# Storing the last rows of a transformer step from 128 partitions: the sample's output as one folded tile

## The chip, the cores and the metric

The kernel runs on one core of one Trainium2 chip. The metric is the device time of one execution in microseconds (us), as a median of several runs. The profile is of one further execution.

## The reference

One layer of a hybrid encoder step is computed for 256 prompt frames and 64 sample frames of width 2048, all in float32. Only its last step bears on the change: the final normalisation of both streams.

```python
def _rmsnorm(x, g):
    xf = x.astype(jnp.float32)
    y = xf * lax.rsqrt(jnp.mean(xf * xf, axis=-1, keepdims=True) + EPS)
    return (y * g.astype(jnp.float32)).astype(x.dtype)
...
    y_prompt = _rmsnorm(xp, final_norm_g)   # (1, 256, 2048)
    y_sample = _rmsnorm(xs, final_norm_g)   # (1, 64, 2048)
```

Before it stand the input projection, the gated branch, the attention branch, the merge and a feed-forward block of 5632 columns. Each output row is 2048 floats, 8 KB.

## The kernel before

The 256 + 64 frames are handled as one block of T = 320 tokens. All large products keep the features on the partitions and the tokens in the free dimension: a weight block of 128x128 is the stationary side, 320 tokens are the moving side, and each weight is split into a high and a low part, so that three products are made for each block (L168 to L170). Weights come from DRAM by the sync queue, ScalarE makes the high part (L135), VectorE the low one (L144). A small calendar (`later`, `pump`) places side work between the products.

The last products are those of w_ffn_down, in column blocks (`DOWN`). The result x2 is kept in `f1` as 16 blocks (m = 0 to 15) of 128 features by 320 tokens. For blocks 0 to 13 the calendar runs, between later products: `out_square` (sum of squares in `acc`), `out_gain` (times final_norm_g) and `out_turn`, which transposes the block on TensorE to token rows (`turn_out`, L895) and copies them from a PSUM bank to the tile `tok` (L908, L909). `tok` is 128 partitions by 3 row groups by 2048 features: row groups 0 and 1 are prompt frames 0 to 127 and 128 to 255, row group 2 holds the 64 sample frames in partitions 0 to 63. `xs` is the list of the three row groups with their heights, (0, 128), (1, 128), (2, 64).

From L941 on the order is written out by hand. `sum_up` (L947) sums the squares over the partitions by a product with a column of ones, for each row group into a PSUM bank of its own, in three calls: for `acc`, for block 14, for block 15. Blocks 14 and 15 are turned in between, their copies to `tok` are made by ScalarE (L905, L906). `sfs` (L969) takes the sums from PSUM to SBUF, and ScalarE's square root with a correction step on VectorE makes `r3`, one factor for each row and row group (L970 to L974).

`scale_out` (L977 to L984) then multiplies a piece of `tok` by its column of `r3`, on VectorE (L983) or ScalarE (L981), and stores it to DRAM on the sync queue or the scalar queue. The order is: row group 0 in two quarters of 512 columns (VectorE, sync queue), first half of row group 1 (ScalarE, scalar queue), first half of the sample (VectorE, sync queue), second half of row group 0 (VectorE, sync queue), second half of row group 1 (ScalarE, scalar queue), second half of the sample (VectorE, scalar queue). These are seven stores. The sync engine waits at the end of the program for all of them (shown as L1043).

Of the kernel before, what the change touches and what calls it, by code (L numbers as in the profile page):

```python
# [12 lines left out]
AF = mybir.ActivationFunctionType  # L13
ALU = mybir.AluOpType
# [4 lines left out]
P = 128  # L19
D = 2048  # L20
DC = D // P
T = 320
TS = 64
F = 5632
FC = F // P
W = 512
EPS = 1e-6
# [43 lines left out]
def tile_hybrid_step(ctx: ExitStack, tc: tile.TileContext, a: dict, outs: list):  # L71
    nc = tc.nc
    y_p, y_s, ko_p, vo_p, ko_s, vo_s, gv_s = outs
# [10 lines left out]
    def bank(name):  # L84
        return psum.tile([P, 512], F32, tag="bank", name=name)
# [94 lines left out]
    ident = main.tile([P, P], F32, name="ident")  # L180
    make_identity(nc, ident)
    ones = main.tile([P, P], F32, name="ones")
# [4 lines left out]
    tok = main.tile([P, 3, D], F32, name="tok")  # L187
# [6 lines left out]
    xs = [(i, P if i < 2 else TS) for i in range(3)]  # L194
# [585 lines left out]
    for g in range(4):  # L780
        ps = gemm(w_bb, g * W, yh, yl, f"bb{g}")
        for t in range(4):
            m = 4 * g + t
# [48 lines left out]
    for g in range(4):  # L832
        ps = gemm(w_ba, g * W, yh, yl, f"ba{g}")
        for t in range(4):
            m = 4 * g + t
# [21 lines left out]
    for g in range(4):  # L857
        ps = gemm(w_out, g * W, xh, xl, f"wo{g}")
        for t in range(4):
            m = 4 * g + t  # L860
# [30 lines left out]

    def turn_out(m, src):
        pt = bank(f"y_{m}")
        for i, n in xs:
            nc.tensor.transpose(pt[:n, i * P : (i + 1) * P], src[:, i * P : i * P + n], ident)  # L895
        return pt

    def out_turn(m, pt=None):
        c = slice(m * P, (m + 1) * P)
        act = pt is not None  # L900
        if not act:
            pt = turn_out(m, f1[:, m, :])
        pv = pt[:, 0:256].rearrange("p (i c) -> p i c", i=2)
        if act:
            nc.scalar.activation(tok[:, 0:2, c], pv, AF.Copy)  # L905
            nc.scalar.activation(tok[0:64, 2, c], pt[0:64, 256:384], AF.Copy)  # L906
        else:
            nc.vector.tensor_copy(tok[:, 0:2, c], pv)  # L908
            nc.vector.tensor_copy(tok[0:64, 2, c], pt[0:64, 256:384])  # L909

    f0 = 0
    for nf in FPARTS:
        for g in range(nf // 4):
            c0 = f0 * P + g * W
            ps = gemm(w_fg, c0, yh, yl, f"fg{f0 + 4 * g}")
            sg = tmp.tile([P, 4, T], F32, tag="st", name=f"sg_{f0 + 4 * g}")
            for t in range(4):
                nc.vector.tensor_tensor(sg[:, t, :], ps[t], r2, op=ALU.mult)
                nc.scalar.activation(sg[:, t, :], sg[:, t, :], AF.Silu)
            ps = gemm(w_fu, c0, yh, yl, f"fu{f0 + 4 * g}")  # L920
            for t in range(4):
                e = tmp.tile([P, T], F32, tag="e1", name=f"h_{f0 + 4 * g + t}", bufs=4)
                nc.vector.tensor_tensor(e, ps[t], r2, op=ALU.mult)
                later(1 + t, lambda m=4 * g + t, e=e, s=sg[:, t, :]: act(m, e, s))
        last = f0 + nf == FC
        for c0, nt in DOWN[last]:
            ps = gemm(w_fd, c0, xh, xl, f"fd{f0}_{c0}", k0=f0, nk=nf, nt=nt)
            if last and c0 == (DC - 2) * P:
                break
            for t in range(nt):  # L930
                m = c0 // P + t
                nc.vector.tensor_tensor(f1[:, m, :], ps[t], f1[:, m, :], op=ALU.add)
                if last:
                    later(1 + 2 * t, lambda m=m: out_square(m))
                    later(1 + 2 * t, lambda m=m: out_gain(m))
                    later(2 + 2 * t, lambda m=m: out_turn(m))
        f0 += nf
# [2 lines left out]

    ctx.enter_context(tc.manual_schedule())  # L941
    lp = late["pool"]
    pss = [bank(f"pss_y_{i}") for i in range(3)]

    def sum_up(q, j):
        for i, n in xs:
            nc.tensor.matmul(  # L947
                pss[i][:n, 0:2], q[:, i * P : i * P + n], ones[:, 0:2], start=(j == 0), stop=(j == 2)
            )

    sfs = lp.tile([P, 3], F32, name="sfs")
    r3 = lp.tile([P, 3], F32, name="r3")
    nh = lp.tile([P, 3], F32, name="nh")
    nc.vector.memset(sfs, 1.0)
    nc.scalar.activation(scrap, acc[:, 0:1], AF.Sqrt)
    sum_up(acc, 0)
    pts = []
    for j, m in enumerate((DC - 2, DC - 1)):
        x2 = f1[:, m, :]
        nc.vector.tensor_tensor(x2, ps[j], x2, op=ALU.add)  # L960
        sq = tmp.tile([P, T], F32, tag="e1", name=f"ysq_{m}", bufs=4)
        nc.scalar.activation(sq, x2, AF.Square)
        xg = tmp.tile([P, T], F32, tag="e1", name=f"xg_{m}", bufs=4)
        nc.vector.tensor_scalar_mul(xg, x2, vec[:, 48 + m : 49 + m])
        sum_up(sq, 1 + j)
        pts.append(turn_out(m, xg))
    out_turn(DC - 2, pts[0])
    for i, n in xs:
        nc.vector.tensor_scalar(sfs[:n, i : i + 1], pss[i][:n, 0:1], 1.0 / D, EPS, op0=ALU.mult, op1=ALU.add)  # L969
    nc.scalar.activation(r3, sfs, AF.Sqrt)  # L970
    nc.vector.reciprocal(r3, r3)
    nc.vector.tensor_tensor(nh, sfs, r3, op=ALU.mult)
    nc.vector.scalar_tensor_tensor(nh, nh, -0.5, r3, ALU.mult, ALU.mult)
    nc.vector.scalar_tensor_tensor(r3, nh, 1.5, r3, ALU.add, ALU.mult)  # L974
    out_turn(DC - 1, pts[1])

    def scale_out(i, c, eng, queue):  # L977
        n = xs[i][1]
        y = tok[:n, i, c]
        if eng is nc.scalar:  # L980
            nc.scalar.activation(y, y, AF.Copy, scale=r3[:n, i : i + 1])  # L981
        else:
            nc.vector.tensor_scalar_mul(y, y, r3[:n, i : i + 1])  # L983
        queue.dma_start(y_p[0][i * P : (i + 1) * P, c] if i < 2 else y_s[0][:, c], y)  # L984

    h0, h1 = slice(0, D // 2), slice(D // 2, D)
    scale_out(0, slice(0, D // 4), nc.vector, nc.sync)
    scale_out(0, slice(D // 4, D // 2), nc.vector, nc.sync)
    scale_out(1, h0, nc.scalar, nc.scalar)
    scale_out(2, h0, nc.vector, nc.sync)  # L990
    scale_out(0, h1, nc.vector, nc.sync)
    scale_out(1, h1, nc.scalar, nc.scalar)
    scale_out(2, h1, nc.vector, nc.scalar)


# [51 lines left out]
```

## Time and profile before

| what | us |
|---|---|
| median of 3 runs | 1952.28 (1951.65 to 1952.33) |
| the profiled execution, its own time | 1951.71 |
| its span, first to last instruction | 1949.8 |
| granted TensorE clock, mean | 0.997 |

The time of an execution is its span and 1.9 us around it. In the rows further down PE is TensorE (products), PEld its weight loads, DVE is VectorE, ACT is ScalarE; a "q" behind an engine's name is its instruction queue, on which DMA issues and waits stand. All times are counted from the start of the span.

### The profile page before, as it was taken

To read this page: it belongs to the slowest core of one execution; us is meant where nothing else is said; L and a number is where in the kernel's file an instruction comes from. 1 tells how busy PE (TensorE), PEld (TensorE's weight loads), DVE (VectorE), ACT (ScalarE), POOL (GpSimd) and SP (SyncE) were. 2 spreads that over 40 slices of the span, in tenths; PEclk is the share of its full clock that TensorE was granted. 3 is DMA by queue.
4 is the path that set the end of the run, shared out by engine and by line. 5 is a ranking of instruction groups with operands and counts; after the bars stand their busy time and mean duration, and the time that the engine had idled before them with its cause. 6 is when DMAs were issued, how large, how long until landed. Compare 5 with 4: busy or idle time off the path is not lost.

```text
span 1949.8 us, 31855 instructions
## 1 busy us (share of the span) xinstructions
PE 1930.4 (99%) x13207; PEld 1924.3 (99%) x13207; DVE 1042.9 (53%) x1530; ACT 813.4 (42%) x1219; POOL 4.7 (0%) x12
## 2 busy tenths in 40 slices
PE   9999999999999999999999999999999999999997
PEld 9999999999999999999999999999999999999997
DVE  6878887944355544455454444443444444444455
ACT  6666766532233343334443333332333333333343
POOL 0000000000000000000000000000000000000000
PEclk9999999999999999999999999999999999999999
DMA  8566566744444444445445555445555544555443
GB/s 279 158 174 179 163 187 180 223 155 149 149 141 135 146 148 149 149 151 205 151 144 150 151 151 152 152 149 146 150 151 151 152 151 148 146 151 151 152 132 106
DMA packets 171024, 307.41 MB, mean 158 GB/s; under 512 B 11472, under 2 KB 31392, under 8 KB 170688
## 3 DMA queue, kind: packets, MB, share of 16 engines
q1 hardware_dynamic: 166128, 295.67, 49.7%
q10 hardware_dynamic: 4752, 9.72, 1.7%
q8 instruction: 103, 1.69, 0.4%
q14 instruction: 41, 0.34, 0.0%
HBM read 292.15 MB, written 12.45 MB: 156 GB/s over the span
## 4 chain that ended last, share of the span: by engine, by line
PE 92%; DVE 2%; ACT 2%; DMA 2%; issue 1%; SPq 0%; ACTq 0%; DVEq 0%
PE mm_fg L170 5%; PE mm_fd L170 5%; PE mm_fu L170 5%; PE mm_fd L169 5%; PE mm_fu L169 5%; PE mm_fg L169 5%; PE mm_fg L168 5%; PE mm_fu L168 5%; PE mm_fd L168 5%; PE mm_u L168 2%; PE mm_bb L169 2%; PE mm_bb L170 2%; PE mm_ba L168 2%; PE mm_ga L168 2%; PE mm_wo L168 2%; PE mm_wo L169 2%
## 5 line engine op out<-in xcount | busy, mean ns | idle before, releaser
L144 DVE TENSOR_TENSOR lo<-raw,hi 128x1024 fp32r<-128x1024 f32 (+1 forms) x533 | 645.3, 1211 | 660.8 <-ACT hi L135 659.4
L135 ACT ACTIVATE hi<-raw 128x1024 fp32r<-128x1024 f32 (+1 forms) x533 | 559.3, 1050 | 1008.7 <-PE mm_fu L169 188.6
L168 PE MATMUL mm_fd<-xh,hi 128*128 128x320 f32 x704 | 218.2, 310 | 0.0
L168 PE MATMUL mm_fg<-yh,hi 128*128 128x320 f32 x704 | 217.8, 309 | 0.0
L170 PE MATMUL mm_fg<-yh,lo 128*128 128x320 f32 x704 | 217.5, 309 | 0.0
L168 PE MATMUL mm_fu<-yh,hi 128*128 128x320 f32 x704 | 217.5, 309 | 0.0
L169 PE MATMUL mm_fu<-yl,hi 128*128 128x320 f32 x704 | 217.5, 309 | 0.0
L170 PE MATMUL mm_fu<-yh,lo 128*128 128x320 f32 x704 | 217.5, 309 | 0.0
L169 PE MATMUL mm_fg<-yl,hi 128*128 128x320 f32 x704 | 217.5, 309 | 0.0
L170 PE MATMUL mm_fd<-xh,lo 128*128 128x320 f32 x704 | 217.1, 308 | 0.0
L169 PE MATMUL mm_fd<-xl,hi 128*128 128x320 f32 x704 | 217.1, 308 | 0.0
L168 PEld LDWEIGHTS mm_fg<-yh,hi 128*128 128x128 f32 x704 | 132.1, 188 | 0.1
L169 PEld LDWEIGHTS mm_fg<-yl,hi 128*128 128x128 f32 x704 | 132.1, 188 | 0.1
L170 PEld LDWEIGHTS mm_fg<-yh,lo 128*128 128x128 f32 x704 | 132.1, 188 | 0.0
L168 PEld LDWEIGHTS mm_fu<-yh,hi 128*128 128x128 f32 x704 | 132.1, 188 | 0.0
L169 PEld LDWEIGHTS mm_fu<-yl,hi 128*128 128x128 f32 x704 | 132.1, 188 | 0.0
L170 PEld LDWEIGHTS mm_fu<-yh,lo 128*128 128x128 f32 x704 | 132.1, 188 | 0.0
L169 PEld LDWEIGHTS mm_fd<-xl,hi 128*128 128x128 f32 x704 | 132.1, 188 | 0.0
L168 PEld LDWEIGHTS mm_fd<-xh,hi 128*128 128x128 f32 x704 | 132.1, 188 | 0.0
L170 PEld LDWEIGHTS mm_fd<-xh,lo 128*128 128x128 f32 x704 | 132.1, 188 | 0.0
L168 PE MATMUL mm_q<-xh,hi 128*128 128x320 f32 x256 | 81.2, 317 | 0.0
L168 PE MATMUL mm_u<-xh,hi 128*128 128x320 f32 x256 | 80.3, 314 | 0.0
(267 smaller groups left out, 3933.0 us busy)
## 6 DMA issues: line engine op xcount, KB each, us to landing
raw<-in_w_in_dram SPq DMA_DIRECT2D x103, 512.0 KB
raw<-in_w_ffn_gate_dram SPq DMA_DIRECT2D x88, 512.0 KB
raw<-in_w_ffn_up_dram SPq DMA_DIRECT2D x88, 512.0 KB
raw<-in_w_ffn_down_dram SPq DMA_DIRECT2D x82, 512.0 KB
raw<-in_w_gate_dram SPq DMA_DIRECT2D x64, 512.0 KB
raw<-in_w_branch_b_dram SPq DMA_DIRECT2D x32, 512.0 KB
raw<-in_w_branch_a_dram SPq DMA_DIRECT2D x32, 512.0 KB
raw<-in_w_out_dram SPq DMA_DIRECT2D x32, 512.0 KB
```

What stands on the lines that cost most here:

```text
L135: nc.scalar.activation(hi[:, :, :n], raws[j][:, :, :n], AF.Copy)
L144: nc.vector.tensor_tensor(lo[:, :, :n], raws.pop(j)[:, :, :n], f32(parts[j][0][:, :, :n]), op=ALU.subtract)
L168: nc.tensor.matmul(o, hi[:, c, cols], xh[:, k, :], start=(k == 0), stop=False)
L169: nc.tensor.matmul(o, hi[:, c, cols], xl[:, k, :], start=False, stop=False)
L170: nc.tensor.matmul(o, lo[:, c, cols], xh[:, k, :], start=False, stop=(k == nk - 1))
```

## The change

The sample's features 1024 to 2047 go to partitions 64 to 127 of row group 2 of `tok`, beside features 0 to 1023 in partitions 0 to 63. To get them there, `turn_out` transposes for the blocks m = 8 to 15 the tokens 192 to 319 (128 columns, whose upper 64 are the sample) in place of tokens 256 to 319, and the copies in `out_turn` take partitions 64 to 127 of the bank to partitions 64 to 127 of `tok`. `sum_up` makes a fourth group of sums for the tokens 192 to 319 in a fourth bank, so that the factors of the sample are in `sfs` in partitions 64 to 127 too; the memset of `sfs` is gone. The sample is scaled by one VectorE operation of 128x1024 instead of two of 64x1024. It is stored in two pieces of 128 partitions by 512 columns, the first on the sync queue, the second on the scalar queue; the target of each is the output seen as (h t d), with h = 2 halves of the features.

```diff
     def turn_out(m, src):
         pt = bank(f"y_{m}")
-        for i, n in xs:
-            nc.tensor.transpose(pt[:n, i * P : (i + 1) * P], src[:, i * P : i * P + n], ident)
+        for i in range(2):
+            nc.tensor.transpose(pt[:, i * P : (i + 1) * P], src[:, i * P : (i + 1) * P], ident)
+        s0 = 2 * P - m // 8 * TS
+        nc.tensor.transpose(pt[: T - s0, 2 * P : 3 * P], src[:, s0:T], ident)
         return pt
 
     def out_turn(m, pt=None):
+
         c = slice(m * P, (m + 1) * P)
+        r = slice(m // 8 * TS, m // 8 * TS + TS)
+        cs = slice(m % 8 * P, m % 8 * P + P)
...
-            nc.scalar.activation(tok[0:64, 2, c], pt[0:64, 256:384], AF.Copy)
+            nc.scalar.activation(tok[r, 2, cs], pt[r, 256:384], AF.Copy)
         else:
             nc.vector.tensor_copy(tok[:, 0:2, c], pv)
-            nc.vector.tensor_copy(tok[0:64, 2, c], pt[0:64, 256:384])
+            nc.vector.tensor_copy(tok[r, 2, cs], pt[r, 256:384])
...
-    pss = [bank(f"pss_y_{i}") for i in range(3)]
+    pss = [bank(f"pss_y_{i}") for i in range(4)]
 
     def sum_up(q, j):
-        for i, n in xs:
-            nc.tensor.matmul(
-                pss[i][:n, 0:2], q[:, i * P : i * P + n], ones[:, 0:2], start=(j == 0), stop=(j == 2)
-            )
+        for o, c in zip(pss, (0, P, 2 * P, T - P)):
+            n = min(P, T - c)
+            nc.tensor.matmul(o[:n, 0:2], q[:, c : c + n], ones[:, 0:2], start=(j == 0), stop=(j == 2))
...
-    nc.vector.memset(sfs, 1.0)
...
-    for i, n in xs:
-        nc.vector.tensor_scalar(sfs[:n, i : i + 1], pss[i][:n, 0:1], 1.0 / D, EPS, op0=ALU.mult, op1=ALU.add)
+    for i, r in ((0, slice(0, P)), (1, slice(0, P)), (2, slice(0, TS)), (3, slice(TS, P))):
+        nc.vector.tensor_scalar(
+            sfs[r, min(i, 2) : min(i, 2) + 1], pss[i][r, 0:1], 1.0 / D, EPS, op0=ALU.mult, op1=ALU.add
+        )
...
+    def scaled(i, c, eng):
+        y = tok[:, i, c]
+        if eng is nc.scalar:
+            nc.scalar.activation(y, y, AF.Copy, scale=r3[:, i : i + 1])
+        else:
+            nc.vector.tensor_scalar_mul(y, y, r3[:, i : i + 1])
+        return y
+
     def scale_out(i, c, eng, queue):
-        n = xs[i][1]
-        y = tok[:n, i, c]
-        if eng is nc.scalar:
-            nc.scalar.activation(y, y, AF.Copy, scale=r3[:n, i : i + 1])
-        else:
-            nc.vector.tensor_scalar_mul(y, y, r3[:n, i : i + 1])
-        queue.dma_start(y_p[0][i * P : (i + 1) * P, c] if i < 2 else y_s[0][:, c], y)
+        queue.dma_start(y_p[0][i * P : (i + 1) * P, c], scaled(i, c, eng))
...
     scale_out(1, h0, nc.scalar, nc.scalar)
-    scale_out(2, h0, nc.vector, nc.sync)
+    sample = scaled(2, h0, nc.vector)
+    dst = y_s[0].rearrange("t (h d) -> h t d", h=2)
+    nc.sync.dma_start(dst[:, :, 0:W], sample[:, 0:W])
     scale_out(0, h1, nc.vector, nc.sync)
     scale_out(1, h1, nc.scalar, nc.scalar)
-    scale_out(2, h1, nc.vector, nc.scalar)
+    nc.scalar.dma_start(dst[:, :, W : 2 * W], sample[:, W : 2 * W])
```

## Rows read from the trace of the kernel before

**Rows 1.** The page, busy time and share of the span of each engine; granted clock.
```profile
span 1949.8 us, 31855 instructions
PE 1930.4 (99%) x13207; PEld 1924.3 (99%) x13207; DVE 1042.9 (53%) x1530; ACT 813.4 (42%) x1219; POOL 4.7 (0%) x12
PEclk9999999999999999999999999999999999999999
```

**Rows 2.** Chain of waits, its end: start, length, work.
```profile
1937.24 0.56 PE pss_y L947 x6
...
1937.83 0.16 DVE sfs L969
...
1938.01 0.21 ACT r L970
...
1939.05 0.49 DVE tok L983
...
1939.93 1.98 DVE tok L983 x3
```

**Rows 3.** Waits of the sync engine's queue, 1938 to 1949.8: total, times, longest.
```profile
SPq L984 <- DVE tok L983: 17.0, 3, 16.1
SPq L1043 <- DMA out_dram<-tok: 6.2, 3, 3.3
```

**Rows 4.** DMA view, 1940.3 to 1948.6, in 40 slices of 0.21 us; q1 sync, q10 scalar.
```profile
DMA  3999999999999999999498789999989989798520
GB/s 148 375 365 405 375 415 355 484 395 395 375 415 375 316 296 237 237 158 158 99 237 336 316 336 513 375 375 454 434 336 434 454 296 375 217 237 237 197 99 0
DMA packets 880, 2.62 MB, mean 316 GB/s; under 512 B 112, under 2 KB 112, under 8 KB 880
q1 hardware_dynamic: 512, 1.31, 50.9%
q10 hardware_dynamic: 368, 1.31, 43.9%
```

**Rows 5.** Table of stretches: length, busy time by engine, clock, DMA share, GB/s.
```profile
1941.90:1943.00 1.10, 0.00 (x0) 0.00 (x0) 0.01 (x1) 0.00 (x0) 0.00 (x0) 0.50 1.03 395
1943.20:1944.40 1.20, 0.00 (x0) 0.00 (x0) 0.00 (x0) 0.00 (x0) 0.00 (x0) 0.50 1.04 201
1944.60:1947.00 2.40, 0.00 (x0) 0.00 (x0) 0.00 (x0) 0.00 (x0) 0.00 (x0) 0.50 0.97 384
1947.20:1948.20 1.00, 0.00 (x0) 0.00 (x0) 0.00 (x0) 0.00 (x0) 0.00 (x0) 0.50 0.88 238
1948.60:1949.80 1.20, 0.00 (x0) 0.00 (x0) 0.00 (x0) 0.00 (x0) 0.00 (x0) 0.50 0.00 0
```

**Rows 6.** DMA view, 240 to 249: scalar queue's packets, its copies.
```profile
q10 hardware_dynamic: 64, 0.16, 4.8%
...
swp<-qr ACTq DMA_DIRECT2D x4, 40.0 KB
```

**Rows 7.** DMA view, 1940.4 to 1941.7.
```profile
DMA packets 257, 0.49 MB, mean 380 GB/s; under 512 B 16, under 2 KB 16, under 8 KB 257
q1 hardware_dynamic: 257, 0.49, 102.0%
```

**Rows 8.** DMA view, 1942 to 1943.
```profile
DMA packets 96, 0.39 MB, mean 393 GB/s; under 512 B 0, under 2 KB 0, under 8 KB 96
```

**Rows 9.** Timeline, 1934.6 to 1938.5: start, length, engine, line, operation, [idle before].
```profile
1934.63 0.49 DVE L960 TENSOR_TENSOR f<-mm_fd,f 128x320 f32<-128x320 f32 x1 [2.03 <-PE mm_fd L170]
1935.17 0.76 PEld L947 LDWEIGHTS pss_y<-ones,acc 128*128 128x128 f32 x6
1935.51 0.49 DVE L960 TENSOR_TENSOR f<-mm_fd,f 128x320 f32<-128x320 f32 x1
1936.69 0.55 PE L895 MATMUL y<-ident,xg 128*128 128x128 f32 x3
1936.97 0.73 PEld L947 LDWEIGHTS pss_y<-ones,ysq 128*128 128x128 f32 x6
1937.39 0.58 DVE L969 TENSOR_SCALAR sfs<-pss_y 128x1 f32<-128x1 f32 x3 [0.97 <-PE pss_y L947]
```

**Rows 10.** Groups by line and shape, 1868 to 1934: busy us, mean ns.
```profile
L895 PE MATMUL y<-ident,f 128*128 128x128 f32 x28 | 5.3, 272 | 0.0
L895 PEld LDWEIGHTS y<-ident,f 128*128 128x128 f32 x28 | 3.9, 140 | 0.1
L895 PE MATMUL y<-ident,f 128*64 128x128 f32 x14 | 3.8, 272 | 0.0
L895 PEld LDWEIGHTS y<-ident,f 128*64 128x64 f32 x14 | 1.5, 110 | 0.0
```

**Rows 11.** Groups by line and shape, 1938 to 1949.8: busy us, mean ns.
```profile
L983 DVE TENSOR_SCALAR tok<-tok,r 64x1024 f32<-64x1024 f32 x2 | 1.5, 742 | 0.0
L983 DVE TENSOR_SCALAR tok<-tok,r 128x1024 f32<-128x1024 f32 x1 | 0.7, 743 | 0.0
```

**Rows 12.** Timeline, 1939 to 1949.8: ScalarE's second scaling, the queues' DMA issues.
```profile
1939.56 2.93 SPq L984 DMA_DIRECT2D out_dram<-tok  x4
1940.62 1.15 ACT L981 ACTIVATE tok<-tok,r 128x1024 f32<-128x1024 f32 x1 [0.43 <-ACT tok L981]
1941.80 1.51 ACTq L984 DMA_DIRECT2D out_dram<-tok  x2
```

## The prediction

> **What bounds the kernel now.** I read the page first: TensorE is busy for 99% of a 1949.8 us span at full clock [rows 1], and nothing in the change touches the products that fill it. So the change can move the time only in the end, after the last product, and, by a hair, through the transposes in the last products. I went to the end with the chain of waits: it leaves TensorE at 1937.8, runs through the small root chain (sfs, r3) to 1939.0, then through VectorE's scaling operations of L983 [rows 2]. Behind these no engine computes anything; the reader should see that the sync engine's own waits end on the stores of tok, 6.2 us of them [rows 3]. So the end of the program is the landing of the stores, and the question is what the 16 DMA engines do between 1940.4 and 1948.5.
>
> The DMA view of that stretch [rows 4] tells three things. First, all seven stores lie in it: 2.62 MB. Second, of its 880 packets 112 are under 512 B. The rows stored are 128+128+64+128 on the sync queue (448) and 128+128+64 on the scalar queue (320), together 768 data packets, one for each row; 880 - 768 = 112 = 7 x 16. So each store leaves one small closing packet on each DMA engine that it used, and each of the seven used all 16. Third, the rate falls twice, to 99 GB/s in the middle and again at the end, while elsewhere it is near 390.
>
> The table of stretches says where [rows 5]: while the 128-row store of the scalar queue runs alone (1941.9 to 1943.0), 395 GB/s; while the sample's first half runs, a store from partitions 0 to 63 alone, 201 GB/s with the engines as busy as before (1.04); in the last microsecond, with the sample's second half, 238. From 1948.6 on nothing moves, and the program closes in 1.2 us. So 64-partition stores are dear: 262,144 B at 201 GB/s is 1.30 us, at 395 it would be 0.66. This is what the change goes for.
>
> **The change, part by part.** The two sample stores become two stores of 128 SBUF rows of 2 KB each. Their target is written as (h t d): outermost h, with 2 values, then 64 rows t, then 512 floats. Outermost counts are thus 128 on the SBUF side and 2 on the DRAM side. **The decisive unknown is over how many DMA engines such a store is dealt.** No transfer of this trace has unlike outermost counts at its two ends. The nearest rows are the rope exchanges at 240 to 249 us: four copies of 8 partitions, 40 KB each [rows 6]. They leave 64 packets on the scalar queue; 4 x 8 rows are 32 data packets, so 32 closing packets, 8 for each copy. An outermost count of 8 is dealt over 8 engines; 64 and 128 over 16. If a share is an equal cut of the outermost count at both ends, 128 and 2 have only two shares in common: partitions 0 to 63 with h=0, and 64 to 127 with h=1. I therefore take **2 engines**, and, as both stores have one shape, the same two for both; the other end of the range is 16.
>
> The Trainium skill states this rule outright (DMA: Bandwidth & Descriptors, section "Why a DMA increments its semaphore by 16 and not by 1"): the engine count is the largest number up to 16 that divides the slowest dimension of both patterns, and the engines are the lowest-numbered ones. By it both sample stores would sit on the same two engines, and the result would be the forecast below; by the rows alone it would be either that or one of the rivals.
>
> Prices of a packet on one engine. A 2 KB packet: in 1940.4 to 1941.7 the quarter stores keep 16 engines full (102%) and start 257 packets, 16 of them closing ones [rows 7]; 16 x 1.3 us / 241 = 0.086 us. A 4 KB packet: 96 packets in 1942.0 to 1943.0 [rows 8], 16 x 1.0 / 96 = 0.167 us. Bounds for the 2 KB one: half of the 4 KB one, 0.083, and 0.086.
>
> Load of the two engines after the change, if both sample stores fall on the same pair: two quarter stores, 8 + 8 packets of 2 KB, 16 x 0.086 = 1.4; three stores of 512 KB, 8 packets of 4 KB each, 24 x 0.167 = 4.0; the sample's, 64 + 64 packets of 2 KB, 128 x 0.086 = 11.0. Sum **16.4 us**. Before, every engine had 16 x 0.086 + 32 x 0.167 = 6.7 us of work at these prices and took 8.1 (1940.4 to 1948.5), the rest being the slow 64-row packets. So the stores last **+8.3 us** longer. The other 14 engines have 5.4 us of work and finish far earlier.
>
> Where the stores start: sum_up runs for four row groups, not three. Three groups are six weight loads in 0.73 us [rows 9], 0.12 each; two more in each of three calls is 6 x 0.12 = +0.73. They are on the path: TensorE goes from one call to the next without a pause, from 1935.17 to 1937.80, and sfs waits for the last. The fourth sfs operation costs 0.58/3 = 0.19 at most [rows 9]; it is partly covered by waiting for the last sum, I take 0.1 (0 to 0.19). The transposes of the sample load 128 columns, not 64, for 8 of the 16 turns: 140 against 110 ns, the operation itself 272 either way [rows 10]; 8 x 0.03 = +0.2 on a full TensorE.
>
> Edits at nothing: the memset of sfs (VectorE waits 2.0 us for the last product there [rows 9]; without that cover some 0.16); one scaling less on VectorE (0.74 by the 64-row form; 128 rows take 0.743 too [rows 11]): ScalarE's second scaling ends at 1940.62 + 1.15 = 1941.8 [rows 12], and the engines have stores until 1948.5 that hide it. The fourth bank of sums makes 8 with two products and two turned blocks; should a turned block get a product's bank, that one is free after L960 at 1936.0, before the transposes at 1936.69 [rows 9].
>
> Queues: behind the sample's first half on the sync queue stands the 512 KB store of (0, h1); if its issue is held until 64 packets on one engine drain, the two engines have the scalar queue's rows meanwhile, so nothing; without that cover the price is the time from issue to first packet, 1939.56 to 1940.4 [rows 4, 12], 0.84 us, twice at most (1.7). The sample's second half on the scalar queue no longer waits for a later scaling; it stands behind (1, h1) as before.
>
> Sum: 8.3 + 0.73 + 0.1 + 0.2 = **+9.3 us**. The profiled execution took 1951.71, its span 1949.8 with 1.9 around it; the median of the runs, 1952.28, lies 0.6 above it. On the median: **1961.6**. Its own range: 2 KB packets at 0.083 (-0.4) and start terms of 0.5 instead of 1.0 give 1960.6; two uncovered issues give 1963.4.
>
> **The rivals.**
> (a) The stores are dealt over all 16 engines, and the change does what it says: not slower. This decides if the SBUF side alone, 128 rows, sets the shares. For it: every 128-row store of the end does so [rows 4]. Against it: the DRAM side has only two outer blocks. Then each sample store gains 1.30 - 0.66 = 0.64, the last one, by 238 GB/s, 1.10 - 0.66 = 0.44: -1.1 against +1.0 at the start: 1952.2, no change that can be told.
> (b) Two engines for each store, but different pairs. The trace cannot tell which eight engines the rope copies took. Then the fullest engine has 1.4 + 4.0 + 64 x 0.086 = 10.9, +2.8 over 8.1, and with 1.0: +3.8, 1956.1.
> (c) Two engines, and the held queue is not covered: 1963.4, in the forecast's range.
>
> **How the numbers follow.** The forecast with (c) 0.80, (b) 0.05, (a) 0.13, anything else 0.02. About 0.2% (3.9 us) is what a measurement of this kernel can tell from no change: slower is above 1956.2. Slower: the forecast and part of (b), 0.82; same: (a) and the rest of (b), 0.17; faster 0.01, since even all of the 8.1 us of stores holds only 1.4 us above the packets' price. The range reaches from (b) to a little over (c): 1955.8 to 1963.8.
>
> **What the profile after would show.** Right: in the stretch of the stores fewer closing packets, 5 x 16 + 2 x 2 = 84 small ones against 112; 384 KB on each of two engines, seen as a long tail at about 2 x 24 = 48 GB/s for some 8 to 10 us after a short stretch near 390; a store end near 1957.7 and a span near 1959. The sums: eight loads of L947 for each call, and L983 starting some 0.8 us later. Wrong: 112 small packets, or a tail at twice that rate (then (b)), or a tail as long with all engines busy, which would mean slow packets and not few engines.

## The result, and the profile after

The changed kernel takes 1960.93 us (median of 6 runs) against 1951.97 for the kernel before in the same sets: the ratio is 1.0049, with a 95% interval of 1.0036 to 1.0061. It is slower by some 9 us; the prediction was 1961.6, in a range of 1955.8 to 1963.8.

Two lines of the page; the span was 1949.8 before [rows 1]:

```profile
span 1958.6 us, 31867 instructions
PE 1930.0 (99%) x13213; PEld 1923.7 (98%) x13213; DVE 1042.9 (53%) x1529; ACT 813.7 (42%) x1219; POOL 4.7 (0%) x12
```

TensorE did the same work, to 0.4 us. The waits of the sync engine's queue (total, times, longest) grow where the end waits for the stores, from 6.2 us [rows 3] to:

```profile
SPq L1052 <- DMA out_dram<-tok: 15.2, 3, 12.4
```

The DMA view of the stretch that holds all seven stores, 1940.1 to 1957.4, in 40 slices of 0.43 us; it answers to [rows 4]:

```profile
DMA  9999999999896412011111111111111111111110
GB/s 346 379 398 431 398 369 379 350 350 341 322 417 265 114 47 33 9 38 33 38 47 52 52 52 52 52 47 52 52 52 52 47 52 57 57 47 47 52 52 28
DMA packets 980, 2.62 MB, mean 152 GB/s; under 512 B 84, under 2 KB 84, under 8 KB 980
```

The bytes are the same, 2.62 MB. The small packets are 84 and no longer 112: five stores closed on 16 engines and two on 2 each, 5 x 16 + 2 x 2. For 5.6 us the stores run near 370 GB/s; then, after one slice at 114, come some 11 us below 60, most of them between 47 and 57, with a busy share of 1 in 10. The table of stretches (length, busy time by engine, clock, DMA share, GB/s) has the two rates and, between them, a stretch that is slower still:

```profile
1941.90:1943.00 1.10, 0.00 (x0) 0.00 (x0) 0.00 (x0) 0.00 (x0) 0.00 (x0) 0.50 1.00 380
1946.10:1947.70 1.60, 0.00 (x0) 0.00 (x0) 0.00 (x0) 0.00 (x0) 0.00 (x0) 0.50 0.15 33
1948.00:1956.00 8.00, 0.00 (x0) 0.00 (x0) 0.00 (x0) 0.00 (x0) 0.00 (x0) 0.50 0.13 50
```

A share of 0.13 is 2 engines of 16, busy without a pause: 50 GB/s is 25 from each.

The start of the stores, in the timeline (start, length, engine, line; L953 is sum_up, L972 sfs, L987 the scaling on VectorE):

```profile
1934.10 1.08 PEld L953 LDWEIGHTS pss_y<-ones,acc 128*128 128x128 f32 x8
...
1935.10 1.05 PEld L953 LDWEIGHTS pss_y<-ones,ysq 128*128 128x128 f32 x8
...
1936.35 1.04 PEld L953 LDWEIGHTS pss_y<-ones,ysq 128*128 128x128 f32 x8
...
1937.52 0.16 DVE L972 TENSOR_SCALAR sfs<-pss_y 64x1 f32<-64x1 f32 x1 [0.16 <-PE pss_y L953]
...
1938.74 1.55 DVE L987 TENSOR_SCALAR tok<-tok,r 128x512 f32<-128x512 f32 x3
```

Eight weight loads for each call where there were six [rows 9], 1.04 to 1.08 us where it was 0.73 to 0.76, and the fourth sfs operation waits for the last of them.

### The profile page after: what moved, and what is told of

Read it like the earlier page. It is cut to its first block, busy times and chain, and to the rows that moved or that the text cites. A ratio compares the mean times of both kernels' runs of the same rounds, so it can differ in the third digit from the quotient of the medians.

```text
span 1958.6 us, 31867 instructions
## 1 busy us (share of the span) xinstructions
PE 1930.0 (99%) x13213; PEld 1923.7 (98%) x13213; DVE 1042.9 (53%) x1529; ACT 813.7 (42%) x1219; POOL 4.7 (0%) x12
## 4 chain that ended last, share of the span: by engine, by line
PE 84%; DVE 2%; ACT 2%; DMA 1%; issue 1%; SPq 0%; ACTq 0%; DVEq 0%
PE mm_fg L170 5%; PE mm_fd L170 5%; PE mm_fu L170 5%; PE mm_fd L169 5%; PE mm_fu L169 5%; PE mm_fg L169 5%; PE mm_fu L168 5%; PE mm_fg L168 5%; PE mm_fd L168 5%; PE mm_u L168 2%; PE mm_bb L170 2%; PE mm_bb L169 2%; PE mm_ba L168 2%; PE mm_ga L168 2%; PE mm_wo L168 2%; PE mm_wo L169 2%
```

## The experiments

The question for the runs was the cause of the long tail. The theory: a folded store is dealt over 2 DMA engines, since its target has an outermost count of 2, and both stores sit on the same two. Rivals: the 2 KB rows are slow in themselves; a folded store holds up what stands behind it; the partition side sets the shares and 2 was a special case. In the DMA views below each window holds all stores of its kernel, unless another is named.

**The same rows, dealt over 16 engines.**

```diff
-    nc.sync.dma_start(dst[:, :, 0:W], sample[:, 0:W])
+    nc.sync.dma_start(y_s[0][:, 0:W], sample[0:TS, 0:W])
+    nc.sync.dma_start(y_s[0][:, 2 * W : 3 * W], sample[TS:P, 0:W])
...
-    nc.scalar.dma_start(dst[:, :, W : 2 * W], sample[:, W : 2 * W])
+    nc.scalar.dma_start(y_s[0][:, W : 2 * W], sample[0:TS, W : 2 * W])
+    nc.scalar.dma_start(y_s[0][:, 3 * W : 4 * W], sample[TS:P, W : 2 * W])
```

> The changed kernel, but each of the sample's two stores is issued as two stores of 64 partitions, one for each half of the features: the same 256 rows of 2 KB, the same queues, only the target's outermost count is 64 and no longer 2. Theory (few engines): nine stores close with 9 x 16 = 144 small packets; every engine has 32 x 0.086 + 24 x 0.167 = 6.8 us of work, some of it slow as it comes from 64 partitions; the tail at 50 GB/s is gone, the stores last 7 to 8.5 us where the changed kernel's took 17, and the time is 1952 to 1953.5. Rival (the 2 KB rows, or rows strided over the target, are what is slow): the rows are the same, so the time stays near 1961.

Measured: 1952.40 us against 1951.90, ratio 1.0004 (0.9995 to 1.0014). DMA view, 1942.0 to 1950.0:

```profile
GB/s 195 379 358 410 359 389 420 420 451 410 410 348 369 328 246 195 123 164 236 451 389 410 389 410 318 328 328 277 328 369 338 369 440 410 369 328 287 236 123 10
DMA packets 1040, 2.62 MB, mean 328 GB/s; under 512 B 144, under 2 KB 144, under 8 KB 1040
```

The same 256 rows of 2 KB, with 9 x 16 closing packets, last 8.0 us with all others and not 17.3. The whole loss is gone, so it lay in the dealing and not in the rows, the fold of the tile or the added sums, which are all still there. This is the run that shows the cause.

**One store folded, the other dealt over 16,** each in turn. In the first run the second store is replaced:

```diff
-    nc.scalar.dma_start(dst[:, :, W : 2 * W], sample[:, W : 2 * W])
+    nc.scalar.dma_start(y_s[0][:, W : 2 * W], sample[0:TS, W : 2 * W])
+    nc.scalar.dma_start(y_s[0][:, 3 * W : 4 * W], sample[TS:P, W : 2 * W])
```

In the second run the first one is:

```diff
-    nc.sync.dma_start(dst[:, :, 0:W], sample[:, 0:W])
+    nc.sync.dma_start(y_s[0][:, 0:W], sample[0:TS, 0:W])
+    nc.sync.dma_start(y_s[0][:, 2 * W : 3 * W], sample[TS:P, 0:W])
```

> The first folded store stays, the second is issued as two stores of 64 partitions. Theory (both folded stores lie on the same two engines, one packet at a time): the fullest engines lose 64 packets of 2 KB and get 8 back, 56 x 0.086 = 4.8 us less: about 1956, with 6 x 16 + 16 + 2 = 114 small packets less or more, and a tail at 50 GB/s some 4 to 5 us long. Rival (each folded store has a pair of its own): the remaining one still needs its 64 x 0.086 on top of the rest, so the time stays within 1 us of the changed kernel's, 1960 to 1961.

> The mirror of the run with one folded store: here the first piece is issued as two stores of 64 partitions and the second stays folded. Theory (a folded store costs its 64 packets on two engines, whichever it is): 114 small packets and the time of the other run within 1 us, 1956 to 1958. Rival (the first one costs more, since others stand behind it on its queue): 1953 to 1955.

Measured: 1957.32 (1.0034, 1.0020 to 1.0047) with the first folded, 1957.26 (1.0031, 1.0020 to 1.0042) with the second. DMA views, 1941.3 to 1954.6 and 1941.5 to 1955.3:

```profile
GB/s 302 394 351 394 456 394 394 357 370 376 357 363 363 376 339 296 333 265 216 290 111 62 74 68 43 12 0 31 31 37 49 49 55 49 49 68 49 25 25 12
DMA packets 1010, 2.62 MB, mean 197 GB/s; under 512 B 114, under 2 KB 114, under 8 KB 1010
```

```profile
GB/s 321 374 386 386 422 392 380 386 208 125 220 368 463 362 356 380 338 404 321 148 30 36 6 24 47 47 59 47 47 59 47 59 48 53 48 53 47 53 30 18
DMA packets 1010, 2.62 MB, mean 190 GB/s; under 512 B 114, under 2 KB 114, under 8 KB 1010
```

114 is 7 x 16 + 2. Each against the kernel before in its own set, none folded costs 0.5 us, one 5.4 or 5.8, and two 9.0: the prices nearly add, as they must when both lie on the same engines. With a pair of engines each, taking one away would have left the time at 1960. The first run came out 1.3 us above the 1956 that was expected: the sum by packets gives 11.6 us of stores, and they lasted 13.3 and 13.8.

**The folded stores behind all others.** The sync queue's one is moved behind the 512 KB store of row group 0.

```diff
-    nc.sync.dma_start(dst[:, :, 0:W], sample[:, 0:W])
     scale_out(0, h1, nc.vector, nc.sync)
     scale_out(1, h1, nc.scalar, nc.scalar)
+    nc.sync.dma_start(dst[:, :, 0:W], sample[:, 0:W])
     nc.scalar.dma_start(dst[:, :, W : 2 * W], sample[:, W : 2 * W])
```

> Both folded stores are issued behind all others. Theory (the price is the work of two engines): the work of these two is the same 16.4 us and they are never without a packet, so the time is the changed kernel's within 1 us, 1960 to 1962; the other stores land early, near 1947, and only the two folded ones land at the end. Rival (a folded store in the middle of a queue holds up the stores behind it, and that is what costs): with nothing behind them the time falls by several us.

Measured: 1961.17 (1.0053, 1.0038 to 1.0068). DMA view, 1939.7 to 1957.3:

```profile
GB/s 312 382 382 414 400 400 382 419 400 400 400 428 56 19 9 42 42 23 19 28 51 51 51 51 51 51 51 51 51 51 51 51 51 51 51 51 51 51 51 28
DMA packets 980, 2.62 MB, mean 149 GB/s; under 512 B 84, under 2 KB 84, under 8 KB 980
```

All prompt stores are through in some 5.5 us, and the time is the same: what counts is the work of the two engines, not what stands behind them.

**Both folded stores on the sync queue,** one behind the other, in one execution.

```diff
     nc.sync.dma_start(dst[:, :, 0:W], sample[:, 0:W])
+    nc.sync.dma_start(dst[:, :, W : 2 * W], sample[:, W : 2 * W])
     scale_out(0, h1, nc.vector, nc.sync)
     scale_out(1, h1, nc.scalar, nc.scalar)
-    nc.scalar.dma_start(dst[:, :, W : 2 * W], sample[:, W : 2 * W])
```

> The changed kernel with both folded stores on the sync queue, one behind the other; all else as it was. The two engines have the same 16.4 us. Theory A: the hole stays, as the prompt stores end beside the first folded store: 17 to 17.6 us from first to last packet. Theory B: without a second queue on the two engines the hole goes: 16.4 to 16.7 us. In both the execution takes 1960 to 1962.

Measured: 1963.69 us in one execution, 1.7 over the upper end of what was expected. The stores are not the reason: the sums start 2.97 us later than in the profile of the changed kernel, so the products before them ended later in this execution. Below are the first sums, then the issue of the 512 KB store that stands behind both folded ones on the sync queue:

```profile
1937.07 1.08 PEld L953 LDWEIGHTS pss_y<-ones,acc 128*128 128x128 f32 x8
...
1945.44 6.16 SPq L991 DMA_DIRECT2D out_dram<-tok  x1
```

The issue of the same store in the changed kernel, where one folded store stands before it:

```profile
1941.14 1.12 SPq L991 DMA_DIRECT2D out_dram<-tok  x1
```

DMA view, 1943.1 to 1960.7:

```profile
GB/s 368 391 382 442 354 410 373 358 326 163 56 47 42 23 14 33 28 42 47 28 233 410 391 205 56 47 56 47 56 47 56 47 56 47 56 47 51 56 56 19
DMA packets 980, 2.62 MB, mean 149 GB/s; under 512 B 84, under 2 KB 84, under 8 KB 980
```

The holding is real behind two folded stores: the issue stands on the queue for 6.16 us, the store comes only in slices 20 to 23, some 9 us after the first packet, and for 4 us before that two engines work and fourteen have next to nothing. But the two have something all the time, and the stores last 17.6 us against 17.3. The held queue cost next to nothing here, since the engines that end last were fed.

**Other outermost counts.** To see the rule and not only its case of 2, the sample is stored as two halves of 64 partitions, and the target's rows are taken with 4, then with 8 blocks outermost. The sample's rows land in another order by this. The diff is against the kernel with two halves, further down; r is 8 in the second run.

```diff
-    nc.sync.dma_start(y_s[0][:, h0], sample[0:TS])
-    nc.scalar.dma_start(y_s[0][:, h1], sample[TS:P])
+    rows = y_s[0].rearrange("(q r) d -> r q d", r=4)
+    nc.sync.dma_start(rows[:, :, h0], sample[0:TS])
+    nc.scalar.dma_start(rows[:, :, h1], sample[TS:P])
```

> The kernel with two halves of 64 partitions and 4 KB rows, but the target's rows are taken as (r q) with 4 blocks outermost, so that the sample's rows land at permuted places; packets, bytes and queues are the same. Theory (the engines are as many as the largest common cut of both outermost counts, 64 and 4 here): each half closes with 4 small packets, 5 x 16 + 2 x 4 = 88 in all; 16 packets of 4 KB for each half on each of 4 engines, 1.4 + 4.0 + 32 x 0.167 = 10.7 us on the fullest engine against 6.7, a tail near 100 GB/s, and a time of 1955 to 1957. Rival (the SBUF side alone sets the shares, and 2 blocks were a case of its own): 112 small packets and 1951 to 1952.5.

> The same with 8 blocks outermost, again with the sample's rows at permuted places. Theory: 5 x 16 + 2 x 8 = 96 small packets; 8 packets of 4 KB for each half on each of 8 engines, 1.4 + 4.0 + 16 x 0.167 = 8.1 us on the fullest engine: 1 us over the version with all 16, 1952 to 1953.5, hardly to be told from the kernel before. Rival: 112 small packets.

Measured: 1958.57 (1.0036, 1.0023 to 1.0049) with 4, 1953.14 (1.0011, 1.0001 to 1.0020) with 8. DMA views with 4: all stores, 1939.5 to 1953.7, then a stretch of the tail, 1947 to 1952; with 8: all stores, 1938.6 to 1948.8, then 1945 to 1948:

```profile
DMA packets 856, 2.62 MB, mean 185 GB/s; under 512 B 88, under 2 KB 88, under 8 KB 856
...
DMA packets 131, 0.50 MB, mean 99 GB/s; under 512 B 10, under 2 KB 10, under 8 KB 131
```

```profile
DMA packets 864, 2.62 MB, mean 257 GB/s; under 512 B 96, under 2 KB 96, under 8 KB 864
...
DMA packets 173, 0.60 MB, mean 199 GB/s; under 512 B 27, under 2 KB 27, under 8 KB 173
```

88 is 5 x 16 + 2 x 4, 96 is 5 x 16 + 2 x 8, and the tails run at 99 and 199 GB/s: 4 and 8 engines at 25 each. The target's outermost count sets the number of engines, though the partition side has 64 rows. The Trainium skill's rule (DMA: Bandwidth & Descriptors, section "Why a DMA increments its semaphore by 16 and not by 1"), the largest number up to 16 that divides both slowest dimensions, agrees with the trace for 128 and 2, 64 and 4, 64 and 8. In all three the smaller count divides the larger, so these runs can't tell that rule from one that takes the smaller count. The time with 4 is 1.6 us over the upper end of what was expected: 14.2 us of stores, where the packets' price gives 10.7. With 8 the time is in the range, but the stores lasted 10.2 us where the price gives 8.1.

**The fold without the few engines.** Two stores of 64 rows of 4 KB, one on each queue, and the sums for three groups.

```diff
-        for o, c in zip(pss, (0, P, 2 * P, T - P)):
+        for o, c in zip(pss, (0, P, T - P)):
...
-    nc.sync.dma_start(dst[:, :, 0:W], sample[:, 0:W])
+    nc.sync.dma_start(y_s[0][:, h0], sample[0:TS])
+    nc.scalar.dma_start(y_s[0][:, h1], sample[TS:P])
```

> The fold without the few engines: partitions 0 to 63 are stored as one store of 64 rows of 4 KB on the sync queue, partitions 64 to 127 as another on the scalar queue at the same place; the sums are made for three groups, as in the kernel before, and the sample's factors are copied to both halves of the partitions by a fourth small VectorE operation. Theory: 7 x 16 = 112 small packets, the two halves run beside each other so that the packets are not slow: engines have 16 x 0.086 + 32 x 0.167 = 6.7 us, the stores last 6.9 to 7.3 us against 8.1 before; the start of the scaling is 0.2 later: 1951 to 1952, the kernel before or 1 us below it. Rival (64-partition stores are slow whatever runs beside them): stores as long as before, 8.1, and 1952.2.

Measured: 1951.71 (1.0001, 0.9991 to 1.0011), no change that can be told. Stretches of this kernel (a 128-row store, then the two halves), and the stores, 1942.0 to 1950.3:

```profile
1943.60:1944.60 1.00, 0.00 (x0) 0.00 (x0) 0.00 (x0) 0.41 (x1) 0.00 (x0) 0.50 1.05 401
1944.80:1946.00 1.20, 0.00 (x0) 0.00 (x0) 0.00 (x0) 0.00 (x0) 0.00 (x0) 0.50 0.95 246
```

```profile
DMA packets 880, 2.62 MB, mean 316 GB/s; under 512 B 112, under 2 KB 112, under 8 KB 880
```

The theory fails here on its second half. The dealing is as expected, 112, but the stores last 8.3 us and not 7. The stretch of the halves has 246 GB/s, little over the 201 of one half alone [rows 5] and far from 401, and its DMA view by queue, 1944.8 to 1946.0, shows that the two scarcely ran together:

```profile
DMA packets 83, 0.29 MB, mean 246 GB/s; under 512 B 11, under 2 KB 11, under 8 KB 83
q1 hardware_dynamic: 59, 0.24, 83.2%
q10 hardware_dynamic: 24, 0.06, 12.0%
```

Both halves were issued at 1942.2, but the sync queue's packets (q1) took 83.2% of the engines' time and the scalar queue's (q10) 12.0%: the halves went mostly one behind the other. So even without the few engines this form of the fold wins nothing; what two halves that move in step would give, no run shows. The Trainium skill says the like (SBUF — State Buffer, section "Can I just issue two DMAs to hit both halves?"): two transfers, at partitions 0 and 64, were only a little faster than one.

**The folded stores alone.**

```diff
     def scale_out(i, c, eng, queue):
-        queue.dma_start(y_p[0][i * P : (i + 1) * P, c], scaled(i, c, eng))
+        scaled(i, c, eng)
```

> The changed kernel with the five prompt stores left out (the prompt's output is not written); the two folded stores stand alone, 128 packets of 2 KB on each of two engines, 128 x 0.084 = 10.8 us by the price of the steady tail. What it asks: in the changed kernel the stores lasted 17.3 us against 16.4 by the packets' price, with a stretch at 33 GB/s after 6 us. Theory A (the prompt stores ending beside the folded ones make packets slow): alone, the two last 10.8 to 11.1 us at 50 GB/s without a hole. Theory B (two folded stores on two queues hinder each other as the second starts): a hole stays, 11.5 to 12.5 us.

Measured: 1958.37 us in one execution. DMA view, 1943.5 to 1955.1, and two stretches:

```profile
GB/s 28 14 14 42 14 42 14 42 42 42 56 49 49 56 42 56 56 42 56 49 49 56 42 56 56 42 56 49 49 56 42 56 49 49 56 49 49 56 42 28
DMA packets 260, 0.52 MB, mean 45 GB/s; under 512 B 4, under 2 KB 4, under 8 KB 260
```

```profile
1943.50:1946.00 2.50, 0.00 (x0) 0.00 (x0) 0.00 (x0) 0.00 (x0) 0.00 (x0) 0.50 0.13 27
1946.00:1954.50 8.50, 0.00 (x0) 0.00 (x0) 0.00 (x0) 0.00 (x0) 0.00 (x0) 0.50 0.13 51
```

4 small packets, 2 for each store. A fifth of the bytes, 0.52 MB, takes 11.6 us on two engines, longer than all 2.62 MB took on sixteen. The packets by queue, first of this run, 1943.5 to 1946.8, then of the run with one queue, 1948.5 to 1950.5:

```profile
DMA packets 52, 0.11 MB, mean 32 GB/s; under 512 B 0, under 2 KB 0, under 8 KB 52
q10 hardware_dynamic: 52, 0.11, 12.6%
```

```profile
DMA packets 21, 0.05 MB, mean 27 GB/s; under 512 B 1, under 2 KB 1, under 8 KB 21
q10 hardware_dynamic: 7, 0.02, 9.6%
q1 hardware_dynamic: 14, 0.03, 3.7%
```

Neither theory on the slow stretch holds. Against A: without any prompt store the slow stretch stays. Against B, although 11.6 us lies in its range: in this run only the scalar queue's store moves for the first 3.3 us, so that no second one hinders it, and with both folded stores on one queue there is a slow stretch too. In that one the folded store's 14 packets took 0.085 us each, near the price in the steady tail (3.7% of what 16 engines have in 2.0 us, shared by 14), and the scalar queue's 7, the end of a prompt store in 4 KB packets, 0.44 on the mean, where a 4 KB packet had taken 0.167 in the kernel before [rows 8]. So it is not always the folded store that is slow, and the cause stays open.

## Why the prediction was right

**The dealing.** The step that decided was to read the closing packets: 7 x 16 before [rows 4], 8 for each copy of 8 partitions [rows 6], and from them that 128 and 2 have two shares in common. 84 packets after, 88 and 96 with 4 and 8 blocks, and the lost time back with 144 show it. That both stores use the same two engines was assumed; the tail at 50 GB/s, where four engines would have given 100, and the two runs with one folded store show it.

**The length of the stores.** Forecast 16.4 us against 8.1; the window that holds them all is 17.3 long against 8.2 (1940.4 to 1948.6). They end at 1957.4, where 1957.7 was forecast. This term was put some 0.8 us too low, and that is the rest of two errors that partly cancel. The price of a packet was a little high: in the steady tail 50 to 52 GB/s on two engines is 0.079 to 0.082 us for 2 KB, below the bounds of 0.083 to 0.086, and 0.5 to 0.9 us less for the 128 packets. So 1.4 to 1.8 us of the 17.3 went beyond the packets. About 1 us of it, by estimate, is what the slices from 1946.2 to 1949.2 lack against 52 GB/s; nothing in the trace of before had shown such a stretch. Where the rest went is not shown.

**The start.** Forecast +0.73 for the sums and +0.1 for sfs. From the first sum to the first scaling it is 1939.05 - 1935.17 = 3.88 before [rows 2, 9] and 1938.74 - 1934.10 = 4.64 after: +0.76. The last sfs operation is hidden behind the last sum, all but 0.03.

**The transposes.** Forecast +0.2. The weight loads did grow, as the groups by shape from 1866 to 1934 show:

```profile
L897 PEld LDWEIGHTS y<-ident,f 128*64 128x64 f32 x8 | 0.9, 110 | 0.0
L897 PEld LDWEIGHTS y<-ident,f 128*128 128x128 f32 x6 | 0.9, 144 | 0.0
```

But the products of this execution ended 1.07 us earlier than those of the profiled execution before (1934.10 against 1935.17, the first sum's start): executions differ by more than this term, and it stays unproven.

**The sum.** In the two profiled executions: -1.07 for the products, +0.76 for the start, +9.1 for the stores, together +8.8, which is 1958.6 - 1949.8. Forecast +9.3; the medians differ by 8.96. The closeness owes something to luck: the stores were put 0.8 too low, and the products happened to be 1 us shorter. The upper figure of 1963.4 is a slip of 0.1 (1961.6 + 1.7), on which nothing rests.

**The edits at nothing.** The scaling saved on VectorE bought no time, as the stores outlast it by far. The wait of a held queue was priced at 0 to 1.7. In the changed kernel the issue behind the folded store took 1.12 us and the two engines had work meanwhile; with both folded stores on one queue it took 6.16, and all stores together lasted 0.3 us longer. So the price at the lower end, nothing, was right.

**The rivals.** (a), 16 engines, is out by the count of 84. Its gain of 1.1 us was not tested as such: the two halves dealt over 16 engines gained nothing, but they ran mostly one behind the other. (b), two pairs, is out by the 50 GB/s and by the runs with one folded store.

## What to carry to other kernels

Read a store's access pattern at both ends before it is fused: with 2, 4 and 8 blocks outermost in DRAM it was dealt over 2, 4 and 8 DMA engines, though 128 or 64 partitions stood at the other end, and a fold written as "(h t d)" with h = 2 left fourteen of sixteen idle. In all these runs the packets under 512 B in a stretch told the number of engines that the stores used, and the rate of the tail, some 25 GB/s for each engine, told it again. At the end of a kernel, where nothing hides the stores, the engine with the most packets is the critical path, and the mean rate says nothing of it.

## What the runs showed of the hardware

Two engines with packets to move do not always reach 50 GB/s: 27 for 2.5 us with the folded stores alone, then 51; 33 for 1.6 us in the changed kernel, then 50; 27 for 2.0 us with one queue. With 4 engines the stores lasted 3.5 us more than their packets' price, with 8 engines 2.1, with one folded store 1.7 and 2.2. With 16 engines they lasted 1.4 more in the kernel before and 1.2 in the run with the same rows, so not all of this belongs to few engines. Neither the second queue nor the prompt stores beside it is the cause by the two runs made; what it is stays open.

A queue can be held behind stores with few engines: the issue behind two folded ones took 6.16 us, where behind one it took 1.12, and the store moved its first bytes some 9 us after the first packet of all; for the last 4 us of that fourteen engines had next to nothing.

Two 64-partition stores from opposite halves of the partitions, issued together on two queues, went mostly one behind the other: a stretch of 246 GB/s with 83.2% of the engines' time for one queue and 12.0% for the other, where one store alone has 201 and a 128-partition store 395 to 401.
